# The mLSTM by chunks with a state, four GLA levels by blocks of 32 tokens, and another end of the program

## The chip, the core and the metric

The program runs on one core of a Trainium2 chip. The core has TensorE for matrix products (PE in the profile, PEld its weight loads), VectorE (DVE), ScalarE (ACT), GpSimd (POOL) and SyncE (SP), which issues most transfers. Each engine takes its own instructions in the order of the program, and the engines meet at semaphores. The metric is the device time of one launch in microseconds. Three runs of the kernel before gave 953.68, 954.08 and 954.04 us, median 954.04.

## What is computed

One decoder layer over 512 tokens of width 1024, all in float32: three token mixers side by side (mLSTM, GLA and gated DeltaNet, each with 4 heads of 128), merged by sigmoid gates, then a squared-ReLU MLP and a last RMSNorm. What the change touches, from the reference:

```python
def mlstm_chunk(carry, xs):                      # per head, chunk of tokens
    b = jnp.cumsum(lf, axis=-1)
    D = jnp.where(causal, b[..., :, None] - b[..., None, :] + li[..., None, :], -jnp.inf)
    inter = b + m[..., None]
    m_t = jnp.maximum(inter, jnp.max(D, axis=-1))
    P = jnp.exp(D - m_t[..., None]) * jnp.einsum('bhtk,bhsk->bhts', q, k)
    w_inter = jnp.exp(inter - m_t)
    num = jnp.einsum('bhts,bhsv->bhtv', P, v) + w_inter[..., None] * jnp.einsum('bhtk,bhkv->bhtv', q, C)
    den = jnp.sum(P, axis=-1) + w_inter * jnp.einsum('bhtk,bhk->bht', q, n)
    h = num / jnp.maximum(jnp.abs(den), jnp.exp(-m_t))[..., None]
    ...
    C = w_old[..., None, None] * C + jnp.einsum('bhsk,bhsv->bhkv', k * w_s[..., None], v)

def gla_chunk(S, xs):                            # a decay for each channel k
    b = jnp.cumsum(g, axis=2)
    diff = b[:, :, :, None, :] - b[:, :, None, :, :]
    decay = jnp.exp(jnp.where(causal[:, :, None], diff, -jnp.inf))
    A = jnp.einsum('bhtsk,bhsk->bhts', q[:, :, :, None, :] * decay, k)
    o = jnp.einsum('bhts,bhsv->bhtv', A, v) + jnp.einsum('bhtk,bhkv->bhtv', q * jnp.exp(b), S)

def rmsnorm(x, g):                               # the last one ends the program
    y = x32 * lax.rsqrt(jnp.mean(x32 * x32, axis=-1, keepdims=True) + EPS)
    return (y * g.astype(jnp.float32)).astype(x.dtype)
```

## The kernel before

Tokens stand on partitions or in columns in blocks of 128. Every large product (projections, gates, up and out projections, both MLP layers) is done as three matmuls of a high and a low float32r part, 128x128 weights by 512 columns; below they are called large matmuls. The small products of the mixers are plain float32, and each of their matmuls appears in the trace as two records; a transpose on TensorE (`tr`) appears as one.

The program is not written in the order in which it runs. `write_block` records operations in a graph, `Graph.schedule` places them by a planner with costs for each kind, and `emit` writes them out. The large matmuls come in the fixed order of `plan`. Everything else on TensorE is slipped between them, as what is called a visit here: a run of small float32 matmuls between two large ones. Small matmuls that wait for another engine are planned at least 1.5 us (`SLACK`) after their input. PSUM tiles of the small products come from a pool of 4 (`mps`). Since all operations are recorded by one helper, every row of the profile names the helper's line, and rows are told apart by tile names.

- mLSTM, `gen_mlstm(h)`: one causal product over all 512 tokens. For each block j of keys, `mqk` is one matmul of 512, 384, 256 or 128 columns (keys of block j by all later queries), `me` its weights exp(...) times the product. Then `mn` sums over the causal blocks: 1+2+3+4 = 10 matmuls of 129 columns (128 values and the normaliser).
- GLA, `gen_gla(h)`: inside a chunk of 128 the decay is split in seven levels, L = 64, 32, 16, 8, 4, 2, 1; each pairs the second half of a run of 2L tokens with its first half. `lw` holds the decayed keys, `lwq` the decayed queries, `ll` their product, which ends up in `lAT`. Levels 64, 32 and 16 are computed by runs (weights of 65, 33 or 17 columns). Levels 8, 4, 2 and 1 take, for each of 4 chunks, one matmul of 128 weight columns by 64 columns, and `copy_predicated` on VectorE picks what belongs to the level. The level of a head has its own PSUM tile.
- The gated DeltaNet, `gen_gdn`, goes chunk by chunk with a state already: `pks`, `pqs`, `pvn`, `pu`, `po`.
- The end, `mlp_last` and `finish(t)`: token blocks t = 0 to 3 get their last MLP product (`mop` for t = 2 and 3), are added to the residual in `x2`, squared with a sum on ScalarE (`fsq`), and scaled by y = 1/rms and the gain `gf`, and stored. The scaling of t = 0 to 2 is one VectorE instruction with both factors per half row (`x<-x,fy,gf`); for t = 3 the gain is multiplied ahead and y is applied on both engines.

Of the kernel before, what the change touches and what calls it, by code (L numbers as in the profile page):

```python
# [7 lines left out]
F32 = mybir.dt.float32  # L8
# [6 lines left out]
P = 128  # L15
D = 1024
S = 512
# [96 lines left out]
class Graph:  # L114
# [92 lines left out]
    def cost(self, eng, method, a, k, op):  # L207
# [10 lines left out]
        if eng == "tensor":  # L218
            if method == "transpose":
                return max(0.109, n / 1200), 0.2  # L220
            if a[1].t.dt == F32R:
                return max(0.112, n / 2400 + 0.0135), 0.2
            return 2 * max(a[1].shape[-1] / 1200, n / 1200, 0.012) + 0.007, 0.2
# [348 lines left out]
def write_block(nc, xT, w_cm, w_tm, w_sc, w_up, w_out, w_mi, w_mo, w_lr, prm, cst, g_fin, x_tm, out):  # L572
# [560 lines left out]
    def gen_mlstm(h):  # L1133
# [61 lines left out]
    hlT = []  # L1195
    cone = slot("cone")
# [8 lines left out]
    def gen_gla(h):  # L1205
        if h == 0:
# [3 lines left out]
            nc.gpsimd.memset(cone, 1.0)  # L1210
            nc.gpsimd.memset(h4(cone)[:, :, 0:1], 0.0)
# [33 lines left out]
        for li_, L in enumerate((64, 32, 16, 8, 4, 2, 1)):  # L1245
            nb = S // (2 * L)
            b3 = b.rearrange("p (n x) -> p n x", x=2 * L)
            w = nc.tile("w", [P, S], F32, f"lw{h}{L}")
            w3 = w.rearrange("p (n x) -> p n x", x=2 * L)
            k3 = lk[h].rearrange("p (n x) -> p n x", x=2 * L)  # L1250
            q3 = lq[h].rearrange("p (n x) -> p n x", x=2 * L)
            nc.vector.tensor_sub(w3[:, :, :L + 1], b3[:, :, L:L + 1].broadcast_to([P, nb, L + 1]), b3[:, :, :L + 1])
            if L > 1:
                nc.vector.tensor_sub(w3[:, :, L + 1:], b3[:, :, L + 1:], b3[:, :, L:L + 1].broadcast_to([P, nb, L - 1]))
            nc.scalar.activation(w, w, AF.Exp, scale=-1.0 / 16.0)
            q_ = q3[:, :, L:]
            if L > 1:
                wq = nc.tile("mq", [P, 256], F32, f"lwq{h}{L}").rearrange("p (n l) -> p n l", l=L)
                nc.vector.tensor_mul(wq, w3[:, :, L:], q_)
                q_ = wq  # L1260
            nc.vector.tensor_mul(w3[:, :, :L + 1], w3[:, :, :L + 1], k3[:, :, :L + 1])
            pl = mps(f"ll{h}{L}")
            p4 = pl[:, :256].rearrange("p (c n l) -> p c n l", c=4, l=L)
            nh = 64 // L
            if L >= 16:
                for c in range(4):
                    for i in range(nh):
                        o = c * P + i * 2 * L
                        mm(p4[i * 2 * L:i * 2 * L + L + 1, c, i], w[:, o:o + L + 1], q_[:, c * nh + i])
# [4 lines left out]
                for i in range(nh):  # L1274
                    r0 = i * 2 * L
                    nc.either.copy(A4[r0:r0 + L + 1, :, r0 + L:r0 + 2 * L], p4[r0:r0 + L + 1, :, i])
            else:
# [401 lines left out]
```

## Time and profile before

| | |
|---|---|
| median of 3 runs | 954.04 us |
| the profiled execution, its own time | 953.96 us |
| its span in the profile | 952.1 us |
| TensorE busy | 942.1 us, 99% |
| VectorE, ScalarE, GpSimd busy | 647.3, 458.5, 4.3 us |
| mean granted TensorE clock | 0.996 of full speed |
| last matmul starts | 942.9 us |

The chain that ended last, followed back from the last instruction, says which engine's work made the time. Along TensorE its pieces run from the start of one group to the start of the next, so that a piece's length by its count is the time that each record took of TensorE, while the durations of single matmuls overlap (a large matmul lasts 0.39 us and the next starts 0.23 us after it).

### The profile page before, as it was taken

How to read it: one execution, taken by the hardware profiler on the slowest of the kernel's cores; microseconds unless marked ns; L12 is line 12 of the kernel's file. 1: busy time of each engine (PE TensorE's matmuls, PEld its weight loads, DVE VectorE, ACT ScalarE, POOL GpSimd, SP SyncE). 2: the span in 40 equal slices, each digit the busy share in tenths (PEclk: the TensorE clock that was granted, in tenths of full speed). 3: DMA queues.
4: the chain of work that ended last, by engine and by line, in shares of the span. 5: the costliest groups of instructions: out<-in, count | busy, mean ns of one | idle time of the engine just before them, and what ended most of it. 6: DMA issues, size and time to landing. Idle time of an engine off the chain costs nothing.

```text
span 952.1 us, 12788 instructions
## 1 busy us (share of the span) xinstructions
PE 942.1 (99%) x4890; PEld 786.2 (83%) x4890; DVE 647.3 (68%) x1146; ACT 458.5 (48%) x877; POOL 4.3 (0%) x18
## 2 busy tenths in 40 slices
PE   9999999999999999999999999999999999999996
PEld 8888888888888888888888888888888888888885
DVE  6766766777725755877735754556778687876886
ACT  6545465543533664455333334455446446545533
POOL 0000000000000000000000000000000000000000
PEclk9999999999999999999999999999999999999998
DMA  9222524122411422222233223213241335424002
GB/s 347 107 90 102 164 89 133 56 78 89 119 67 45 178 89 89 89 67 67 90 111 111 89 94 105 89 45 115 87 149 60 122 111 177 134 88 133 1 1 89
DMA packets 37941, 96.74 MB, mean 102 GB/s; under 512 B 7884, under 2 KB 12108, under 8 KB 37880
## 3 DMA queue, kind: packets, MB, share of 16 engines
q1 hardware_dynamic: 37592, 95.62, 30.4%
q8 instruction: 38, 0.62, 0.3%
q10 hardware_dynamic: 288, 0.30, 0.1%
q14 instruction: 23, 0.19, 0.1%
HBM read 93.27 MB, written 2.65 MB: 101 GB/s over the span
## 4 chain that ended last, share of the span: by engine, by line
PE 99%; DVE 0%; DVEq 0%; issue 0%
PE mip L533 18%; PE pp L533 9%; PE upp L533 7%; PE P L533 6%; PE wop L533 5%; PE mop L533 3%; PE mvp L533 3%; PE lrp L533 2%; PE dzp L533 2%; PE lvp L533 2%; PE ll L533 2%; PE gt21p L533 1%; PE gt13p L533 1%; PE gt20p L533 1%; PE gt22p L533 1%; PE gt12p L533 1%
## 5 line engine op out<-in xcount | busy, mean ns | idle before, releaser
L533 DVE TENSOR_TENSOR em<-em 128x1024 f32<-128x1024 f32 x28 | 34.1, 1219 | 0.1
L533 ACT ACTIVATE A<-rl 128x256 f32<-128x256 f32 x64 | 23.7, 411 | 3.2 <-DVE aS4l L533 2.0
L533 DVE SCALAR_TENSOR_TENSOR sg<-sg,upp 128x512 f32<-128x512 f32 x24 | 16.5, 686 | 11.9 <-PE upp L533 11.7
L533 DVE TENSOR_TENSOR lw<-lbs 128x260 f32<-128x260 f32 (+12 forms) x52 | 20.9, 448 | 4.9 <-PE ll L533 4.9
L533 ACT ACTIVATE rl<-mip 128x512 f32<-128x512 f32 x32 | 18.9, 590 | 6.3 <-PE mip L533 6.3
L533 DVE TENSOR_TENSOR P<-P,pp 128x512 f32<-128x512 f32 x24 | 16.2, 686 | 7.6 <-PE pp L533 7.4
L533 ACT ACTIVATE lw<-lw 128x512 f32<-128x512 f32 x28 | 17.6, 630 | 7.9 <-DVE lw L533 7.3
L533 PEld LDWEIGHTS ll<-lwq,lw 128*17 128x17 f32 (+3 forms) x320 | 17.5, 131 | 3.8 <-ACT lAT L533 1.8
L533 PE MATMUL ll<-lwq,lw 128*17 128x16 f32 (+3 forms) x320 | 18.2, 214 | 0.0
L533 DVE SCALAR_TENSOR_TENSOR x<-pp,r2c,x 128x512 f32<-128x512 f32 x24 | 16.9, 745 | 0.0
L533 DVE TENSOR_TENSOR x2T<-xr,wop 128x512 f32<-128x512 f32 x8 | 5.5, 687 | 16.3 <-PE wop L533 16.3
L533 ACT ACT_TABLE_LOAD x10 | 12.8, 1283 | 1.3 <-PEq L1667 1.2
L533 DVE TENSOR_TENSOR lw<-lw,lks 128x260 f32<-128x260 f32 (+6 forms) x28 | 13.1, 497 | 0.0
L533 DVE SCALAR_TENSOR_TENSOR x<-pp,r2n,x 128x512 f32<-128x512 f32 x14 | 10.5, 748 | 3.1 <-PE pp L533 3.1
L533 ACT COPY lAT<-ll 17x64 f32<-17x64 f32 (+3 forms) x32 | 7.1, 231 | 10.8 <-PE ll L533 10.4
L533 ACT ACTIVATE yh<-sg 128x512 fp32r<-128x512 f32 x8 | 5.0, 632 | 13.5 <-DVE sg L533 13.5
L533 DVE TENSOR_TENSOR me<-me,mqk 128x512 f32<-128x512 f32 (+3 forms) x16 | 7.7, 484 | 5.4 <-PE mqk L533 4.9
L533 ACT ACTIVATE fsq<-x 128x512 f32<-128x512 f32 (+1 forms) x9 | 5.3, 585 | 12.5 <-DVE x L533 12.5
L533 PEld LDWEIGHTS mn<-mv,me 128*128 128x128 f32 x80 | 10.0, 191 | 1.1 <-DVE smo L533 0.2
L533 DVE TENSOR_TENSOR sg<-sg,sg 128x512 f32<-128x512 f32 x16 | 10.8, 690 | 0.1
L533 PE MATMUL mqk<-mqs,mks 128*128 128x512 f32 (+3 forms) x32 | 10.7, 432 | 0.0
L533 ACT ACTIVATE cvs<-cv 128x512 f32<-128x512 f32 x12 | 7.5, 629 | 6.1 <-DVE cv L533 6.0
(1849 smaller groups left out, 3276.1 us busy)
## 6 DMA issues: line engine op xcount, KB each, us to landing
em<-in_w_mo_dram SPq DMA_DIRECT2D x28, 512.0 KB, 3.3
xk<-in_xT_dram SPq DMA_DIRECT2D x8, 256.0 KB, 5.3
em<-in_x_tm_dram SPq DMA_DIRECT2D x4, 512.0 KB, 8.4
em<-scr_rows SPq DMA_DIRECT2D x16, 128.0 KB, 5.0
xr<-in_xT_dram SPq DMA_DIRECT2D x8, 256.0 KB, 4.0
out_dram<-x SPq DMA_DIRECT2D x7, 256.0 KB, 2.4
nm<-scr_rows SPq DMA_DIRECT2D x4, 256.0 KB, 4.6
mo00r<-in_w_tm_dram SPq DMA_DIRECT2D x1, 512.0 KB
```

Of the source, the lines that this page charges most:

```text
L533: getattr(getattr(nc, eng), method)(*[f(x) for x in a], **{n: f(x) for n, x in k.items()})
```

## The change

1. `gen_mlstm` keeps the causal product inside each chunk of 128 and carries a state `C` from chunk to chunk. Per head: a transpose of three chunks of the keys (`mkt`), scaled on VectorE into `kt`; four `mqk` of 128 columns into one PSUM tile; three `mu` = keys by values of 129 columns; `C` built from `mu` by one copy and two VectorE instructions; the queries scaled by exp in `qe`; and 4 + 3 = 7 `mn` instead of 10. Small scalars of the state go through `x` (`mx`). The rows of exp and of the masks are as long as before for the blocks that remain.
2. `gen_gla` goes through the levels in the groups (64), (32, 16), (8, 4), (2, 1); the levels of a group share a PSUM tile. Levels 8 to 1 are 16 matmuls of 32 weight columns by 16 columns instead of 4 of 128 by 64: each reaches its own 32 partitions of the result. What they don't write is read by `copy_predicated`, so that ScalarE copies zeros into the PSUM tile first (512 columns, two per head). `nc.after` lets a group's products begin when the keys of its last level are there.
3. The end: t = 0 and 1 get the gain on GpSimd and y on ScalarE (`nc.scalar.mul`) instead of both on VectorE; a square root on a single column (`root`) ahead brings the table load forward.
4. The planner's cost of a small matmul of at most 16 columns by at most 33 weight columns is 0.033 us. The planner's order of all engines changes with this.

```diff
+            if n <= 16 and a[1].shape[-1] <= 33:
+                return 0.033, 0.2
...
-        pt = []
-        for j in range(4):
-            e = nc.tile("w", [P, S], F32, f"me{h}{j}")
-            bias = a_c[:, h, j:j + 1]
-            nc.scalar.activation(e[:, blk(j)], md[:, blk(j)], AF.Exp, bias=bias)
-            if j < 3:
-                nc.scalar.activation(e[:, (j + 1) * P:], nm[:, (j + 1) * P:], AF.Exp, bias=bias)
-            pq = mps(f"mqk{h}{j}")
-            mm(pq[:, j * P:], mk[h][:, blk(j)], mq[h][:, j * P:])
-            nc.vector.tensor_mul(e[:, j * P:], e[:, j * P:], pq[:, j * P:])
-            pt.append(e)
+
+        end = h4(nm)[:, :, P - 1]
+        x = small("mx", 16)
+        nc.vector.tensor_add(x[:, 0:3], a_c[:, h, 0:3], end[:, 0:3])
+        nc.vector.tensor_sub(x[:, 3:5], end[:, 1:3], end[:, 0:2])
+        nc.vector.tensor_scalar_mul(x[:, 8:11], end[:, 0:3], -1.0)
+        nc.scalar.activation(x[:, 0:5], x[:, 0:5], AF.Exp)
+        kt, e, qe, C = (nc.tile("w", [P, S], F32, f"m{n}{h}") for n in ("kt", "e", "qe", "C"))
+
+        pk = mps(f"mkt{h}")
+        for c in range(3):
+            tr(pk[:, blk(c)], mk[h][:, blk(c)])
+        nc.vector.tensor_mul(h4(kt)[:, :3], h4(pk)[:, :3], bc(x[:, 0:3]))
+        for c in range(4):
+            nc.scalar.activation(e[:, blk(c)], md[:, blk(c)], AF.Exp, bias=a_c[:, h, c:c + 1])
+        pq = mps(f"mqk{h}")
+        for c in range(4):
+            mm(pq[:, blk(c)], mk[h][:, blk(c)], mq[h][:, blk(c)])
+        nc.vector.tensor_mul(e, e, pq)
+        for c in range(1, 4):
+            nc.scalar.activation(qe[:, blk(c)], nm[:, blk(c)], AF.Exp, bias=x[:, 7 + c:8 + c])
+        nc.vector.tensor_mul(qe[:, P:], qe[:, P:], mq[h][:, P:])
+        pu = mps(f"mu{h}")
+        for c in range(3):
+            mm(pu[:, blk(c, P + 1)], kt[:, blk(c)], mv[c][:, h, :])
+        nc.either.copy(C[:, :P + 1], pu[:, :P + 1])
+        for c in (1, 2):
+            nc.vector.scalar_tensor_tensor(C[:, blk(c, P + 1)], C[:, blk(c - 1, P + 1)], x[:, 2 + c:3 + c], pu[:, blk(c, P + 1)], op0=ALU.mult, op1=ALU.add)
...
-                for j in range(t + 1):
-                    mm(n2[:, tt], pt[j][:, blk(t)], mv[j][:, h, :], start=(j == 0), stop=(j == t))
+                mm(n2[:, tt], e[:, blk(t)], mv[t][:, h, :], start=True, stop=(t == 0))
+                if t:
+                    mm(n2[:, tt], qe[:, blk(t)], C[:, blk(t - 1, P + 1)], start=False, stop=True)
...
+    zero = slot("zero", n=512)
...
+            nc.gpsimd.memset(zero, 0.0)
...
-        for li_, L in enumerate((64, 32, 16, 8, 4, 2, 1)):
+        for levels in ((64,), (32, 16), (8, 4), (2, 1)):
...
+            pl = mps(f"ll{h}{levels[0]}")
+            if levels[0] < 16:
+
+                nc.scalar.copy(pl[:, :256 * len(levels)], zero[:, :256 * len(levels)])
+
+            def prod(o, a, q_):
+
+                nc.after(lw[levels[-1]])
+                mm(o, a, q_)
...
+                    else:
+                        for i in range(4):
+                            n0 = c * nh + i * m
+                            prod(p4[blk(i, 32), c, i * m:(i + 1) * m], w[:, blk(4 * c + i, 32)], q_[:, n0:n0 + m])
...
-                for c in range(4):
-                    mm(p4[:, c], w[:, blk(c)], q_[:, c * nh:(c + 1) * nh])
-                nc.vector.copy_predicated(At.rearrange("p (c n x) -> p c n x", c=4, x=2 * L)[:, :, :, L:], lmask(li_ - 3), p4)
...
+                    nc.vector.copy_predicated(At.rearrange("p (c n x) -> p c n x", c=4, x=2 * L)[:, :, :, L:], lmask((8, 4, 2, 1).index(L)), p4)
...
+            if t < 2:
+                nc.gpsimd.tensor_mul(o, o, gf[hf])
...
-                nc.vector.scalar_tensor_tensor(x2[t][hf], x2[t][hf], y, gf[hf], op0=ALU.mult, op1=ALU.mult)
+                if t < 2:
+                    nc.scalar.mul(x2[t][hf], x2[t][hf], y)
+                else:
+                    nc.vector.scalar_tensor_tensor(x2[t][hf], x2[t][hf], y, gf[hf], op0=ALU.mult, op1=ALU.mult)
...
+    root = small("root", 1)
+    nc.follow(prev[1][1])
+    nc.scalar.activation(root, r2c[:, 0:1], AF.Sqrt)
```

How the built programs stand, without times. In both, 3705 large matmuls follow in the same order of stages. Before there are 104 visits of small matmuls among them, after 111.

**TensorE, one visit with small GLA levels of heads 0, 1 and 2, before.** `ll` is the PSUM tile, `lw` the weights, `lwq` or `lqs` the queries; 128x64 is the shape of the result; the large matmuls around it are of the gate projection.

```order
L533 MATMUL ll_4203<-lqs_2293,lw_3828 128x64
L533 MATMUL ll_4205<-lwq_4145,lw_4124 128x64 x4
L533 MATMUL ll_4203<-lqs_2293,lw_3828 128x64 x2
L533 MATMUL ll_4218<-lwq_4165,lw_4130 128x64 x4
L533 MATMUL ll_4227<-lqs_2335,lw_4021 128x64
L533 MATMUL ll_4203<-lqs_2293,lw_3828 128x64
L533 MATMUL ll_4227<-lqs_2335,lw_4021 128x64 x3
```

The same engine after, at level 8 and level 4 of head 0: one group of 16 between large matmuls, and the next split by level 64 of head 1.

```order
L535 MATMUL gt13p_3864<-xh,gt130h 128x512
L535 MATMUL ll_3849<-lwq_3412,lw_3358 32x16 x16
L535 MATMUL gt13p_3864<-xh,gt130l 128x512
...
L535 MATMUL ll_3849<-lwq_3836,lw_3365 32x16 x11
L535 MATMUL ll_3957<-lwq_3917,lw_3861 65x64 x4
L535 MATMUL ll_3957<-lqs_2364,lks_2945 1x1 x4
L535 MATMUL ll_3849<-lwq_3836,lw_3365 32x16 x5
```

There are 16 such groups of 16 in the program, in 16 visits, four of which hold other small matmuls too; the 64 matmuls of 128x64 are gone.

**TensorE, the first head's mLSTM, before:** products of all later queries, then (30 rows on) the sums over blocks.

```order
L533 MATMUL mqk_1442<-mqs_1319,mks_861 128x512
L533 MATMUL mqk_1450<-mqs_1319,mks_861 128x384
L533 MATMUL mqk_1455<-mqs_1319,mks_861 128x256
...
L533 MATMUL mn_1539<-mv_111,me_1420 128x129
L533 MATMUL mn_1539<-mv_113,me_1428 128x129
L533 MATMUL mn_1539<-mv_115,me_1433 128x129
```

The same engine after:

```order
L535 MATMUL mkt_1353<-cs,mks_861 128x128 x3
L535 MATMUL mkt_1358<-cs,mks_904 128x128 x3
L535 MATMUL mq0p_1317<-xh,mq01l 128x512
...
L535 MATMUL mqk_1378<-mqs_1325,mks_861 128x128 x4
...
L535 MATMUL mu_1401<-mv_111,mkt_1366 128x129
L535 MATMUL mu_1401<-mv_113,mkt_1366 128x129
L535 MATMUL mu_1401<-mv_115,mkt_1366 128x129
```

Six large matmuls stand between `mkt` and `mqk`, three between `mqk` and `mu`, some nine more until the first `mn`.

**ScalarE, the end of the program, before.** x_5438, x_5614, x_5426 and x_5602 are the halves of t = 0 and 1; x_5433 and x_5609 of t = 2, x_5455 and x_5631 of t = 3.

```order
L533 ACTIVATE fsq,fss<-x_5602 128x512
L533 ACTIVATE fsq,fss<-x_5433 128x512
L533 ACT_TABLE_LOAD
L533 ACTIVATE fs<-fss,fe 128x1 x2
L533 ACTIVATE fsq,fss<-x_5609 128x512
L533 ACTIVATE fs<-fss,fe 128x1
L533 ACTIVATE fsq,fss<-x_5455 128x512
```

The same engine after; x_5664, x_5840, x_5652 and x_5828 are now the halves of t = 0 and 1, x_5659 and x_5835 of t = 2, x_5681 of t = 3:

```order
L535 ACTIVATE fs<-fss,fe 128x1 x2
L535 ACTIVATE fsq,fss<-x_5659 128x512
L535 ACTIVATE x_5664<-x_5664,fy 128x512
L535 ACTIVATE x_5840<-x_5840,fy 128x512
L535 ACTIVATE x_5652<-x_5652,fy 128x512
L535 ACTIVATE fsq,fss<-x_5835 128x512
L535 ACTIVATE x_5828<-x_5828,fy 128x512
```

Four multiplications by y stand on ScalarE among the squares, and four fewer on VectorE; the table load moved ahead of the first square. On GpSimd, the four multiplications by the gain follow an ISA instruction (a reload of its library) that the program before does not have. ScalarE also has 14 table loads instead of 10, the four new ones in the softplus of the GLA: two beside the `lvp` and two beside the `dzp` projection.

## Rows read from the trace of the kernel before

**Rows 1.** The page: busy us, share of span, instructions; shares of the chain.

```profile
PE 942.1 (99%) x4890; PEld 786.2 (83%) x4890; DVE 647.3 (68%) x1146; ACT 458.5 (48%) x877; POOL 4.3 (0%) x18
...
PE 99%; DVE 0%; DVEq 0%; issue 0%
```

**Rows 2.** TensorE's waits: who waited for whom, us, times, longest.

```profile
PE mvp L533 <- DVE onem L533: 1.1, 1, 1.1
```

**Rows 3.** Chain, MLP: start us, us until the next piece, what, records.

```profile
646.57 5.44 PE mip L533 x24
```

**Rows 4.** Chain, mLSTM, 154 to 191 us: single products, one head's sums.

```profile
154.80 0.86 PE mqk L533 x2
...
171.84 0.65 PE mqk L533 x2
...
175.66 0.43 PE mqk L533 x2
...
176.78 0.22 PE mqk L533 x2
...
188.65 2.23 PE mn L533 x20
```

**Rows 5.** Chain: four transposes; two steps of the DeltaNet's state.

```profile
157.05 0.44 PE pk L533 x4
...
287.78 0.89 PE pvn L533 x8
288.67 1.38 PE upp L533 x6
```

**Rows 6.** Chain, GLA levels and the large matmuls behind them.

```profile
394.88 0.32 PE ll L533 x32
395.19 1.59 PE gt22p L533 x6
...
412.25 0.74 PE ll L533 x16
...
440.50 3.52 PE ll L533 x32
444.02 6.90 PE gt21p L533 x30
```

**Rows 7.** Chain, 32x32 matmuls of the DeltaNet's solve.

```profile
260.16 1.13 PE pY L533 x64
261.29 3.62 PE gt20p L533 x15
264.91 1.03 PE pT L533 x29
```

**Rows 8.** Stretch of the GLA levels, 385 to 475 us: length, busy of each engine.

```profile
385.00:475.00 90.00, 90.00 (x689) 74.90 (x688) 71.79 (x146) 42.07 (x86) 2.04 (x4) 1.00 0.24 77
```

**Rows 9.** Timeline of the end: start us, us, engine, operation, count, idle time before.

```profile
924.87 0.64 ACT L533 ACTIVATE fsq<-x 128x512 f32<-128x512 f32 x1 [1.33 <-DVE x L533]
...
933.00 0.63 ACT L533 ACTIVATE fsq<-x 128x512 f32<-128x512 f32 x1 [1.94 <-DVE x L533]
...
939.60 0.73 DVE L533 SCALAR_TENSOR_TENSOR x<-x,fy,gf 128x512 f32<-128x512 f32 x1
...
943.24 0.48 DVE L533 SCALAR_TENSOR_TENSOR x<-mop,r2c,x 128x256 f32<-128x256 f32 x1 [0.23 <-PE mop L533]
...
946.40 1.79 DVE L533 SCALAR_TENSOR_TENSOR x<-x,fy,gf 128x512 f32<-128x512 f32 x3
...
946.52 0.72 ACT L533 ACTIVATE x<-x,fy 128x512 f32<-128x512 f32 x1 [1.93 <-DVE fy L533]
...
948.11 0.35 DVE L533 TENSOR_SCALAR x<-x,fy 128x256 f32<-128x256 f32 x1
```

**Rows 10.** Chain, two of the small steps of y at the end.

```profile
944.36 0.15 DVE fv L533
...
945.57 0.18 DVE fs L533
```

More of the change, by code (lines that the diff above doesn't have):

```diff
@@ L1244, in gen_gla @@
         nc.either.copy(lkt[h][:, :3 * P], pk[:, :3 * P])
-        for li_, L in enumerate((64, 32, 16, 8, 4, 2, 1)):
[L1246 to L1265, printed above, removed]
-                for c in range(4):
-                    for i in range(nh):
-                        o = c * P + i * 2 * L
-                        mm(p4[i * 2 * L:i * 2 * L + L + 1, c, i], w[:, o:o + L + 1], q_[:, c * nh + i])
@@ new lines, in gen_gla @@
+        for levels in ((64,), (32, 16), (8, 4), (2, 1)):
+            lw, lq_ = {}, {}
+            for L in levels:
+                nb = S // (2 * L)
+                b3 = b.rearrange("p (n x) -> p n x", x=2 * L)
+                w = nc.tile("w", [P, S], F32, f"lw{h}{L}")
+                w3 = w.rearrange("p (n x) -> p n x", x=2 * L)
+                k3 = lk[h].rearrange("p (n x) -> p n x", x=2 * L)
+                q3 = lq[h].rearrange("p (n x) -> p n x", x=2 * L)
+                nc.vector.tensor_sub(w3[:, :, :L + 1], b3[:, :, L:L + 1].broadcast_to([P, nb, L + 1]), b3[:, :, :L + 1])
+                if L > 1:
+                    nc.vector.tensor_sub(w3[:, :, L + 1:], b3[:, :, L + 1:], b3[:, :, L:L + 1].broadcast_to([P, nb, L - 1]))
+                nc.scalar.activation(w, w, AF.Exp, scale=-1.0 / 16.0)
+                q_ = q3[:, :, L:]
+                if L > 1:
+                    wq = nc.tile("mq", [P, 256], F32, f"lwq{h}{L}").rearrange("p (n l) -> p n l", l=L)
+                    nc.vector.tensor_mul(wq, w3[:, :, L:], q_)
+                    q_ = wq
+                nc.vector.tensor_mul(w3[:, :, :L + 1], w3[:, :, :L + 1], k3[:, :, :L + 1])
+                lw[L], lq_[L] = w, q_
+            pl = mps(f"ll{h}{levels[0]}")
[4 more added lines that the diff above has]
+                mm(o, a, q_)
+            for n, L in enumerate(levels):
+                w, q_ = lw[L], lq_[L]
+                p4 = pl[:, blk(n, 256)].rearrange("p (c n l) -> p c n l", c=4, l=L)
+                nh, m = 64 // L, 16 // L
+                for c in range(4):
+                    if L >= 16:
+                        for i in range(nh):
+                            o = c * P + i * 2 * L
+                            prod(p4[i * 2 * L:i * 2 * L + L + 1, c, i], w[:, o:o + L + 1], q_[:, c * nh + i])
+                    else:
+                        for i in range(4):
+                            n0 = c * nh + i * m
+                            prod(p4[blk(i, 32), c, i * m:(i + 1) * m], w[:, blk(4 * c + i, 32)], q_[:, n0:n0 + m])
@@ L1273, in gen_gla @@
                     nc.either.copy(A4[0:1, :, 0:1], pl[0:1, 256:260].unsqueeze(2))
[L1274 to L1277, printed above, removed]
-                for c in range(4):
-                    mm(p4[:, c], w[:, blk(c)], q_[:, c * nh:(c + 1) * nh])
-                nc.vector.copy_predicated(At.rearrange("p (c n x) -> p c n x", c=4, x=2 * L)[:, :, :, L:], lmask(li_ - 3), p4)
+                if L >= 16:
+                    for i in range(nh):
+                        r0 = i * 2 * L
+                        nc.either.copy(A4[r0:r0 + L + 1, :, r0 + L:r0 + 2 * L], p4[r0:r0 + L + 1, :, i])
+                else:
+                    nc.vector.copy_predicated(At.rearrange("p (c n x) -> p c n x", c=4, x=2 * L)[:, :, :, L:], lmask((8, 4, 2, 1).index(L)), p4)
     lss = one("lss", [P, 16])
@@ L1579, in finish @@
             for hf in range(2):
-                nc.vector.scalar_tensor_tensor(x2[t][hf], x2[t][hf], y, gf[hf], op0=ALU.mult, op1=ALU.mult)
+                if t < 2:
+                    nc.scalar.mul(x2[t][hf], x2[t][hf], y)
+                else:
+                    nc.vector.scalar_tensor_tensor(x2[t][hf], x2[t][hf], y, gf[hf], op0=ALU.mult, op1=ALU.mult)
                 nc.sync.dma_start(out[blk(t), blk(hf, 512)], x2[t][hf])
```

## The prediction

> **What bounds the kernel now.** I read the chain of work that ended last first. TensorE holds 99% of it, and TensorE is busy for 942.1 of the 952.1 us of the span [rows 1]. Busy can hide waits behind long matmuls, so the list of TensorE's waits comes second: it has one entry, 1.1 us at the start [rows 2]. Third come the chain's pieces in the MLP: 24 large matmuls take 5.44 us, 0.2267 us each, without a break [rows 3]. So TensorE is never late for anything, and the time is what TensorE's instructions cost, one after the other, plus what follows the last matmul. A change of TensorE's own work is paid one to one; work on other engines counts only where it makes TensorE wait, or behind the last matmul.
>
> That last stretch is 943.2 to 952.1 us. VectorE works there without a pause on leftovers: from 943.24 until 948.11 + 0.35 = 948.46 us it has the last addition, two multiplications by the gain, four scalings of half rows of t = 1 and 2, and t = 3's own [rows 9]. The last store is issued behind it; the other 3.6 us of the span are that store and the end of the program.
>
> I make the sum against the profiled execution's own 953.96 us; the median of the runs is 954.04, so the two are one number here.
>
> **The mLSTM.** A piece of the chain with its count gives TensorE's price of a record. Before, per head: the four products cost 0.86, 0.65, 0.43 and 0.22 us, together 2.16, and the ten sums 2.23 us for 20 records, 0.1115 each [rows 4]. After, per head: four products of 128x128 are 8 records. Such a record costs 0.89 / 8 = 0.111 us in the DeltaNet's state [rows 5], so 0.89 us. Three transposes cost 3 x 0.11 = 0.33 us [rows 5]. Three `mu` of 129 columns are 6 records, 0.67 us, and seven `mn` are 14 records, 1.56 us, both at the 0.1115 of [rows 4]. That is 3.45 us instead of 4.39, **0.94 us less a head, 3.8 us in all**. The bounds are narrow, 3.5 to 4.0, since every shape stands in the trace.
>
> Around it, VectorE and ScalarE lose some long instructions and gain about as many short ones; neither bounds anything. What it could cost is a wait: keys transposed, scaled, multiplied, `C` built, and only then the sums, four steps over three engines where two stood before. The trace has the same kind of chain in the DeltaNet: there the large matmuls right behind a visit cost 1.38 us for six, 0.23 each, so no wait follows [rows 5], and the list of waits has none there [rows 2]. Six, three and about nine large matmuls lie between a step and the next for the first head; at 0.2267 us that is 1.4, 0.7 and 2 us of cover. I take nothing for it in the sum and keep it as a rival.
>
> **The GLA's four small levels.** Before, the 128 records of 128 weight columns by 64 cost 3.52 us for 32, plus an edge: the thirty large matmuls behind them take 6.90 us instead of 30 x 0.2267 = 6.80. So 3.6 us for a head's 32, 14.4 us in all [rows 6]. After, 512 records of 32 weight columns by 16, in 16 visits of 32. The trace has not this shape, but level 16 comes near: 32 records with 17 weight columns by 16 columns, in the same order over the four groups of 32 partitions. They cost 0.32 us (the piece at 394.88), and the six large matmuls behind them 1.59 instead of 1.36: 0.55 us with the edges [rows 6]. 16 x 0.55 = 8.8 us. Four of the visits share their edges with others, which I leave as an allowance for 32 instead of 17 weight columns. **5.6 us less.** The lower bound of the cost is 0.52 a visit (edges shared), 6.1 us less. The upper one is the row where only two tiles alternate: `pY`, 32x32, costs 1.13 + (3.62 - 3.40) = 1.35 us for 64 records [rows 7], of which the 0.22 is edge, so 0.79 for 32, 12.6 in all: 1.8 us less. I take level 16's price, since its tiles, rows and moving columns are the same and only the weight columns differ.
>
> The Trainium skill has a rule that speaks against this step ("TensorEngine Tiling (Array Packing)", Performance Considerations, Instruction Overhead): a matmul has some 60 cycles of overhead, so that one column lasts as long as sixty, and a dimension that is already small should give no tiling factor. By it 512 short records would each cost an estimated 25 ns and the step would bring next to nothing; level 16's 0.32 us for 32 records is 10 ns each and speaks against the rule here.
>
> Hidden beside TensorE: eight copies of zeros into PSUM on ScalarE, about 0.6 us each by its other instructions of 512 columns [rows 9], 4.7 us more in a stretch where ScalarE is busy for 42.07 of 90 us. VectorE has 71.79 us there and keeps its work [rows 8]; with 5.6 us less of TensorE the stretch is 84.4 us long and VectorE 85% busy. That still covers it; the margin is what the waiting rival eats. The four table loads that ScalarE gains lie beside the `lvp` and `dzp` projections, where hardly a visit stands on TensorE and the wait list is empty [rows 2].
>
> **The end.** Behind the last matmul VectorE keeps the last addition (0.48), one gain multiplication of 256 columns (about the 0.35 of the row of 256), one scaling of 512 (0.73), t = 3's small steps (0.15 and 0.18 in [rows 10], with two reciprocals and a sum that are no longer, some 0.5), and the last half row (0.4 and 0.35): 2.8 us from 943.24, so 946.05 instead of 948.46 [rows 9]. That is 2.4 us. ScalarE's own scaling of t = 3 starts with the same y and ends near 946.2, and two stores of 256 KB then start at once instead of half a microsecond apart, so I take **2.1 us less**, with bounds 0 and 2.4. It rests on t = 0 and 1 being out of the way: GpSimd's multiplications can start with the first square at 924.87 and the last of the four at 933.63 [rows 9], 18 and 10 us ahead of the last matmul's end; the trace has no arithmetic on GpSimd, so I bound it from below by VectorE's 0.73 us for a scaling of as many elements [rows 9], and take twice that. The four scalings on ScalarE, 0.72 us each, fit between its squares, where it idles 1.9 us at a time [rows 9].
>
> **Sum.** 3.8 + 5.6 + 2.1 = 11.5 us; 953.96 - 11.5 = **942.5 us**. With all bounds at their good ends, 4.0 + 6.1 + 2.4, it is 941.5, with the levels' cost at its upper bound 946.3, and with the end's gain gone as well 948.4.
>
> **Rivals.** *TensorE comes to wait.* The mLSTM has 12 new hand-overs and the levels 8 with ScalarE's zeros. If half of them wait for one VectorE instruction of about 0.45 us, 4.5 us come back: 947.0. Against it: today's list of waits is empty with a chain of the same kind in it; for it: the cover of three large matmuls is only 0.7 us.
>
> *The short matmuls don't overlap as level 16's.* Single-column matmuls on one tile show what a short record costs alone: in the 0.74 us of 16 records [rows 6] eight have 64 columns and eight have one; at half of `mqk`'s 0.111 for the former, 0.04 us is left for each of the latter with the edges, 0.025 to 0.035. At 0.03 us, 512 records cost 15.4 us and 16 edges 0.23 each 3.7: 4.7 us more than before in place of 5.6 less, in all 952.8. That would be within 0.2% of before or just faster; the row `pT`, all on one tile, has the same 0.035 us a record [rows 7]. Against it: level 16 has four tiles in turn and 0.010.
>
> *GpSimd is late (slower than before).* ScalarE takes its instructions in order, and the scalings of t = 0 and 1 stand ahead of the squares of t = 2 and 3. If GpSimd's first product comes late, all that ends the program comes late with it. Cover: t = 0 is scaled from 939.60 now, behind the table load that moves ahead, so from some 3 us earlier then; from the first square's end, 925.5, to 936.5, less GpSimd's own 1.4, leaves some 9 us [rows 9]. Each further microsecond is paid in full, and with the 11.5 us won elsewhere the kernel is slower than before from 20 us on; 25 us late gives 958.5. For it: the program now reloads GpSimd's library, which the trace does not price. Against it: the reload stands in GpSimd's queue behind work of the GLA, some 500 us earlier, and may run there. The Trainium skill ("GPSIMD Engine Reference", Instruction dispatch) gives about 6 us for the first call of a freshly loaded kernel; no run here shows it, and it would be covered.
>
> **How the numbers follow.** The forecast, 941.0 to 944.5, has 0.67; waiting, around 947, 0.15; levels between level 16's price and the bound of `pY`, up to 948.4, 0.08; no overlap, about 952.8, 0.04; GpSimd late, 958, 0.04; anything else 0.02. The range is 941.0 to 947.5. A measurement of this kernel tells about 0.2%, 1.9 us, from no change. Faster by more than that: 0.67 + 0.15 + 0.08 + a share of the rest = 0.92; the same 0.04; slower 0.04.
>
> **What would show it.** In the trace after: TensorE's list of waits still almost empty; the visits of 32 `ll` records 0.32 us long as level 16's; eight `mqk` records 0.89 us; the last matmul near 933.8 us; VectorE's last instruction 2.8 us behind it. Wrong it would be if TensorE waits anywhere for more than a microsecond, if an `ll` record costs over 0.02 us, or if ScalarE stands before a scaling of t = 0 or 1 near the end.

## The result, and the profile after

The changed kernel takes 943.31 us (median of four runs, 943.29 to 943.96); the kernel before, beside it, 953.92 us. The ratio is 0.9891, with an interval of 0.9873 to 0.9908: faster, by 10.6 us or 1.1%. The prediction was 942.5 us, range 941.0 to 947.5.

The page after, with the lines that answer to [rows 1]: busy time, share and instructions of each engine, and the shares of the chain that ended last.

```profile
span 941.5 us, 13618 instructions
...
PE 932.8 (99%) x5286; PEld 775.3 (82%) x5286; DVE 651.4 (69%) x1157; ACT 469.6 (50%) x903; POOL 10.7 (1%) x23
...
PE 97%; DVE 2%; ACT 0%; DMA 0%; issue 0%; SPq 0%; DVEq 0%
```

TensorE's waits after, the answer to [rows 2] (who waited for whom, us, times, longest):

```profile
PE mvp L535 <- DVE onem L535: 1.1, 1, 1.1
```

TensorE is busy 9.3 us less, 932.8 for 942.1, although it has 396 records more. Its list of waits still holds the one entry at the start, so none of the new hand-overs is waited for. VectorE's share of the chain went from 0% to 2%: the chain leaves TensorE earlier than it did, at the program's end, which is shown below.

The chain in the mLSTM after (start us, us until the next piece, what, records), the answer to [rows 4]:

```profile
140.01 0.89 PE mqk L535 x8
...
142.26 2.08 PE dk1p L535 x9
144.34 0.45 PE mn L535 x4
...
146.37 0.22 PE mn L535 x2
...
147.30 0.67 PE mu L535 x6
...
148.66 0.33 PE mkt L535 x3
...
151.06 0.89 PE mn L535 x8
```

These are the prediction's prices to the hundredth: four products 0.89, three transposes 0.33, three `mu` 0.67, and 14 records of `mn` 0.45 + 0.22 + 0.89 = 1.56. The sum of a head is 3.45 us, where it was 4.39.

The chain in the GLA after, the answer to [rows 6]:

```profile
418.37 0.32 PE ll L535 x32
...
421.65 0.38 PE ll L535 x32
422.03 1.59 PE gt12p L535 x6
...
435.32 0.92 PE ll L535 x48
...
449.09 1.01 PE ll L535 x45
```

The piece of 0.32 is a level 16, as before. The next one is a level 8 to 1 in its new form: 0.38 us for 32 records, and the six large matmuls behind it cost 1.59 instead of 1.36, so 0.61 with the edge where the prediction took 0.55. The pieces of 48 and 45 records are two of the four visits in which such a level stands with another and pays no edge of its own. 16 x 0.61 less four edges of 0.23 is 8.8 us, the predicted sum: what a visit costs more is what the shared edges give back. The allowance for this was not worked out, so that the two come out equal is luck.

The end, three engines' timelines of the changed kernel (start us, us, engine, operation, count, idle time before and what ended it). First GpSimd and ScalarE:

```profile
916.43 1.55 POOL L535 TENSOR_TENSOR x<-x,gf 128x512 f32<-128x512 f32 x1 [531.47 <-ACT fsq L535]
920.03 1.52 POOL L535 TENSOR_TENSOR x<-x,gf 128x512 f32<-128x512 f32 x1 [2.05 <-ACT fsq L535]
```

```profile
928.17 0.63 ACT L535 ACTIVATE fsq<-x 128x512 f32<-128x512 f32 x1 [0.18 <-DVE x L535]
928.71 0.19 ACT L535 ACTIVATION_READ_ACCUMULATOR fsq<-x 128x1 f32 x1
928.93 1.95 ACT L535 ACTIVATE x<-x,fy 128x512 f32<-128x512 f32 x3
930.79 0.61 ACT L535 ACTIVATE fsq<-x 128x512 f32<-128x512 f32 x1
```

And VectorE, which answers to [rows 9, 10]:

```profile
916.75 1.78 DVE L535 TENSOR_TENSOR z01l<-A,z01h 128x512 fp32r<-128x512 f32 x1
...
919.71 0.68 DVE L535 TENSOR_TENSOR z11l<-A,z11h 128x512 fp32r<-128x512 f32 x1
920.32 1.78 DVE L535 SCALAR_TENSOR_TENSOR x<-u,r2c,x 128x512 f32<-128x512 f32 x1
...
923.88 3.48 DVE L535 SCALAR_TENSOR_TENSOR x<-P,r2c,x 128x512 f32<-128x512 f32 x3
927.28 0.20 DVE L535 TENSOR_SCALAR fe<-fss 128x1 f32<-128x1 f32 x2
927.40 0.73 DVE L535 SCALAR_TENSOR_TENSOR x<-mop,r2c,x 128x512 f32<-128x512 f32 x1
...
929.07 0.73 DVE L535 SCALAR_TENSOR_TENSOR x<-mop,r2c,x 128x512 f32<-128x512 f32 x1
931.53 0.16 DVE L535 TENSOR_TENSOR fv<-fss,fe 128x1 f32<-128x1 f32 x1 [1.73 <-ACT fsq L535]
931.61 0.74 DVE L535 SCALAR_TENSOR_TENSOR x<-mop,r2c,x 128x512 f32<-128x512 f32 x1
...
934.70 0.48 DVE L535 SCALAR_TENSOR_TENSOR x<-mop,r2c,x 128x256 f32<-128x256 f32 x1
...
936.21 0.15 DVE L535 TENSOR_TENSOR fv<-fss,fe 128x1 f32<-128x1 f32 x1
...
936.98 0.48 DVE L535 SCALAR_TENSOR_TENSOR x<-x,fy,gf 128x256 f32<-128x256 f32 x1
937.38 0.35 DVE L535 TENSOR_SCALAR x<-x,fy 128x256 f32<-128x256 f32 x1
```

The last matmul starts at 933.70 and ends at 933.98, where before it ended at 943.20: 9.2 us earlier. From there to the span's end are 7.5 us, where there were 8.95: 1.45 us less, together the span's 10.7. VectorE's last addition starts 0.73 us behind the last matmul (before 0.04), and two things stand ahead of it. At 916.75 and 920.32, while GpSimd multiplies, instructions of VectorE take 1.78 us that took 0.68 and 0.74 before. At 928.93 ScalarE has three scalings of t = 0 and 1 ahead of the second square of t = 2, whose input was there at 929.8. VectorE waits 1.73 us for that square, and the addition for t = 3 stands behind the wait.

Both lie on the chain that ended last. Before, it stays on TensorE until the last matmul; after, it leaves TensorE at 914.80 and goes on over VectorE's stretched instruction ("issue" is time in which the engine waits for nothing that the profile shows), ScalarE's scalings and the square:

```profile
932.17 11.04 PE mop L533 x60
943.22 0.02 issue
```

```profile
911.84 2.96 PE P L535 x13
...
916.84 0.06 DVE z01l L535
916.89 1.56 issue
...
929.57 1.32 ACT x L535 x2
930.89 0.62 ACT fsq L535 x2
```

### The profile page after: what moved, and what is told of

Its sections match the earlier page's. It is cut to its first block, busy times and chain, and to the rows that moved or that the text cites. A ratio compares the mean times of both kernels' runs of the same rounds, so it can differ in the third digit from the quotient of the medians.

```text
span 941.5 us, 13618 instructions
## 1 busy us (share of the span) xinstructions
PE 932.8 (99%) x5286; PEld 775.3 (82%) x5286; DVE 651.4 (69%) x1157; ACT 469.6 (50%) x903; POOL 10.7 (1%) x23
## 4 chain that ended last, share of the span: by engine, by line
PE 97%; DVE 2%; ACT 0%; DMA 0%; issue 0%; SPq 0%; DVEq 0%
PE mip L535 19%; PE pp L535 10%; PE upp L535 7%; PE P L535 5%; PE wop L535 5%; PE lrp L535 3%; PE mvp L535 2%; PE lvp L535 2%; PE dzp L535 2%; PE mop L535 2%; PE ll L535 1%; DVE x L535 1%; PE gt12p L535 1%; PE gt21p L535 1%; PE gt22p L535 1%; PE gt13p L535 1%
## 5 line engine op out<-in xcount | busy, mean ns | idle before, releaser
L535 PEld LDWEIGHTS ll<-lwq,lw 128*32 128x32 f32 (+3 forms) x608 | 9.4, 109 | 6.9 <-issue 5.3
L535 DVE COPY_PREDICATED lAT<-cs,ll 128x256 f32<-128x256 uint8 x16 | 9.3, 583 | 5.3 <-PE ll L535 5.3
L535 ACT COPY lAT<-ll 17x64 f32<-17x64 f32 (+3 forms) x32 | 7.0, 231 | 10.6 <-PE ll L535 10.3
L535 POOL TENSOR_TENSOR x<-x,gf 128x512 f32<-128x512 f32 x4 | 5.9, 1484 | 535.9 <-ACT fsq L535 535.9
L535 PE MATMUL ll<-lwq,lw 128*32 128x16 f32 (+3 forms) x608 | 11.5, 187 | 0.0
L535 DVE TENSOR_TENSOR sg<-sg,sg 128x512 f32<-128x512 f32 x16 | 10.7, 686 | 0.1
L535 DVE TENSOR_TENSOR lwq<-lw,lqs 128x256 f32<-128x256 f32 x24 | 9.8, 423 | 0.3
L535 DVE TENSOR_TENSOR Z<-Z,tmU 64x30 f32<-64x30 f32 (+14 forms) x30 | 9.5, 318 | 0.2
```

The costliest lines, as they stand in the source:

```text
L535: getattr(getattr(nc, eng), method)(*[f(x) for x in a], **{n: f(x) for n, x in k.items()})
```

## The experiments

Theory: three parts, each paid one to one (the first two by TensorE's visits, the third by the distance from the last matmul to the end), and small records cheap because records on different quarters of the array overlap. Rivals: the gain comes from another order of the planner; from the grouping of the levels; the price of a record is its issue or its columns; and for the end, GpSimd's stretch or ScalarE's queue as what kept it short.

The kernels, with the median, the ratio to the kernel before and its interval, and the time from the last matmul's end to the span's end:

| kernel | us | ratio (interval) | behind the last matmul |
|---|---|---|---|
| changed | 943.31 | 0.9891 (0.9873 to 0.9908) | 7.50 |
| old mLSTM | 946.79 | 0.9925 (0.991 to 0.994) | 7.50 |
| old GLA levels | 948.67 | 0.9946 (0.9931 to 0.996) | 7.50 |
| old end | 944.74 | 0.9906 (0.989 to 0.9923) | 8.93 |
| same quarter in a row | 950.59 | 0.9965 (0.9952 to 0.9978) | 7.52 |
| groups, old shapes | 949.02 | 0.9949 (0.9933 to 0.9966) | 7.46 |
| blocks of 64 | 946.75 | 0.9925 (0.9913 to 0.9937) | 7.52 |
| early root alone | 944.45 | 0.9901 (0.9887 to 0.9916) | 8.32 |
| scalings moved | 943.17 | 0.9888 (0.9874 to 0.9901) | 6.99 |
| no product on GpSimd (t = 0 and 1 miss the gain) | 942.71 | 0.9885 (0.9871 to 0.9898) | 6.99 |
| gain on VectorE | 943.33 | 0.9891 (0.9875 to 0.9906) | 7.18 |
| three edits of the end | 942.75 | 0.9885 (0.987 to 0.99) | 6.87 |

Kernels that differ in the end alone end their last matmul between 933.93 and 934.23 us with the same plan for TensorE, so that 0.3 us between two times says nothing of an edit; the last column is steadier.

### One part undone at a time

The mLSTM, as it was:

```diff
-        pu = mps(f"mu{h}")
-        for c in range(3):
-            mm(pu[:, blk(c, P + 1)], kt[:, blk(c)], mv[c][:, h, :])
...
+                for j in range(t + 1):
+                    mm(n2[:, tt], pt[j][:, blk(t)], mv[j][:, h, :], start=(j == 0), stop=(j == t))
```

> The changed kernel with the mLSTM of before (one causal product over all 512 tokens); the GLA's blocks and the new end stay. If the three parts of the change are paid one to one and add up, the time is that of the changed kernel, 943.3 us, plus the 3.8 us of TensorE's visits (bounds 3.5 to 4.0): 947.1 us, and the distance from the last matmul to the end stays 7.5 us. Rival: the chunked mLSTM's gain on TensorE was given back or came from the new order of the large matmuls; then the time stays within 0.7 us of 943.3.

946.79 us, 3.5 more. The distance at the end is unchanged. Its chain has the old prices back, a product of 512 columns and one of 384 among them:

```profile
150.18 0.86 PE mqk L535 x2
...
154.46 0.65 PE mqk L535 x2
```

The rival is out. Of the 3.8 by the prices some 0.3 are missing; the last matmul's end varies by as much between kernels of one plan, and no run says where they went.

The GLA's levels, as they were:

```diff
-        for levels in ((64,), (32, 16), (8, 4), (2, 1)):
+        for li_, L in enumerate((64, 32, 16, 8, 4, 2, 1)):
...
-                            prod(p4[blk(i, 32), c, i * m:(i + 1) * m], w[:, blk(4 * c + i, 32)], q_[:, n0:n0 + m])
+                    mm(p4[:, c], w[:, blk(c)], q_[:, c * nh:(c + 1) * nh])
```

> The changed kernel with the GLA's levels of before (seven levels each with its own PSUM tile, levels 8 to 1 by 128 weight columns and 64 columns, no zeros); mLSTM and end stay as changed. The trace of the changed kernel has 17.8 us for all visits of the levels, that of before 23.3: expected 943.3 + 5.5 = 948.8 us. If the prediction's lower price of a level were the right one it would be 949.4, by its upper one 945.1. Rival: the shorter matmuls brought nothing that the trace's piece lengths can be trusted for; then 943.3.

948.67 us: 5.4 more, between the two bounds and by the level 16's price.

The end, as it was:

```diff
-            if t < 2:
-                nc.gpsimd.tensor_mul(o, o, gf[hf])
...
-                if t < 2:
-                    nc.scalar.mul(x2[t][hf], x2[t][hf], y)
-                else:
-                    nc.vector.scalar_tensor_tensor(x2[t][hf], x2[t][hf], y, gf[hf], op0=ALU.mult, op1=ALU.mult)
+                nc.vector.scalar_tensor_tensor(x2[t][hf], x2[t][hf], y, gf[hf], op0=ALU.mult, op1=ALU.mult)
...
-    nc.scalar.activation(root, r2c[:, 0:1], AF.Sqrt)
```

> The changed kernel with the end of before: VectorE scales t = 0 and 1 with both factors, no product on GpSimd, no scaling of them on ScalarE, no early square root. Last matmul to the end of the span was 8.95 us before and 7.5 us after, so 943.3 + 1.45 = 944.8 us; the prediction's term would give 945.4. Rival: the new end gained nothing of its own (the shorter distance came from the planner's other order): 943.3.

944.74 us, 1.4 more, and the distance is back at 8.93. So the end's part is worth 1.4 us. The three parts undone come to 3.5 + 5.4 + 1.4 = 10.3 of the 10.6: they add up.

### What makes a small record cheap

The same 512 records, the quarter in the outer loop:

```diff
-                for c in range(4):
...
-                        for i in range(4):
+                    for i in range(4):
+                        for c in range(4):
                             n0 = c * nh + i * m
```

> The changed kernel with the same 512 records of levels 8 to 1, but in another order: all four chunks of one group of 32 partitions first, then the next group, so that eight records in a row use the same quarter of the array. If a record is cheap because records on different quarters overlap, it now costs what pT's on one tile cost, 0.035 us: 32 x 0.035 + 0.23 = 1.35 us a visit instead of 0.585, 16 visits 12 us more, about 955.5 us. If a record costs only what its issue costs (7 ns by the changed kernel's trace), the order changes nothing: 943.3. If only the two records of one matmul must follow each other and neighbours overlap anyway, something near the latter.

950.59 us, 7.3 more with not an instruction added. In its chain, the same visits:

```profile
400.62 0.81 PE ll L535 x32
...
420.14 0.32 PE ll L535 x32
...
423.42 0.82 PE ll L535 x32
```

Level 16, in its old order, still costs 0.32; a level of the new form went from 0.38 to 0.81 or 0.82, and 16 x 0.44 = 7.0 us is the loss. A record costs 0.025 us on the average of the piece, with quarters in turn 0.012.

The starts of the single records, which the rows above merge, show why (the visit at 421.58 in the changed kernel's trace, the one at 423.35 in this run's). In both, two records on the same quarter start 0.032 us apart (the first two 0.053). In the changed kernel four quarters run side by side, 0.007 us behind one another, so that four records start every 0.032 us. Here the next quarter's first record starts 0.153 us behind this one's first, when three of its eight are still to start. So the overlap is what pays, and the expectation's mechanism is right. Its price for one quarter was nearly right too: `pT`'s records start 0.032 us apart as well, and its 0.035 is the same with the ends of the piece. What it left out is that quarters still overlap where they change.

The Trainium skill's 60 cycles of overhead for a matmul ("TensorEngine Tiling (Array Packing)", Performance Considerations, Instruction Overhead), an estimated 25 ns, come near this run's average for a record (half of a matmul of the program). But neither pace in the two traces is 25 ns: it is 32 ns on one quarter and 7 ns between quarters in turn. So the rule does not hold here for tiles in turn, and for one tile its figure is low.

The new groups of levels with the old shapes:

```diff
-                        for i in range(4):
-                            n0 = c * nh + i * m
-                            prod(p4[blk(i, 32), c, i * m:(i + 1) * m], w[:, blk(4 * c + i, 32)], q_[:, n0:n0 + m])
+                        prod(p4[:, c], w[:, blk(c)], q_[:, c * nh:(c + 1) * nh])
```

> The changed kernel with the levels in their new groups (shared PSUM tiles, zeros, the wait for the last keys of a group), but levels 8 to 1 by the matmuls of before, 128 weight columns by 64 columns. If the GLA's gain is the price of the short matmuls, it all goes: 16 visits of 0.90 us instead of 0.585 are 5 us more, 948.4 us, as with the whole old GLA. If part of it came from the grouping (fewer visits, fewer edges), the time lies below that; if all of it, 943.3.

949.02 us, 5.7 more: as slow as the whole old GLA. The same visit in its chain:

```profile
425.89 0.84 PE ll L535 x8
```

Grouping, zeros and the wait for the last keys bring nothing by themselves; the short matmuls bring all.

Blocks of 64 tokens:

```diff
-                        for i in range(4):
-                            n0 = c * nh + i * m
-                            prod(p4[blk(i, 32), c, i * m:(i + 1) * m], w[:, blk(4 * c + i, 32)], q_[:, n0:n0 + m])
+                        for i in range(2):
+                            n0 = c * nh + i * 2 * m
+                            prod(p4[blk(i, 64), c, i * 2 * m:(i + 1) * 2 * m], w[:, blk(2 * c + i, 64)], q_[:, n0:n0 + 2 * m])
```

> The changed kernel with levels 8 to 1 by blocks of 64 tokens: 8 matmuls of 64 weight columns by 32 columns for a level, 16 records a visit, two halves of the array in turn, instead of 32 records of 32 by 16 on four quarters. If a record's price is its issue and the pair of halves overlap as pY's two tiles, 16 x 0.0177 + 0.22 = 0.50 us a visit instead of 0.585: 1.3 us less, 942.0 us. If the price follows the columns that the array works on (0.11 us for a record of 128 by 64, so 0.055 for 32 columns and half of that with two in turn), 16 x 0.0275 + 0.2 = 0.64 us: 0.9 us more, 944.2. If two halves in turn do not overlap, 16 x 0.055 + 0.2 = 1.08 us a visit: 8 us more, 951.

946.75 us, 3.4 more, and none of the three times came. A visit's piece in its chain, and the six large matmuls behind it:

```profile
427.85 0.59 PE ll L535 x16
428.44 1.59 PE gt12p L535 x6
```

The price in the second case was right all the same. In the trace two records on one half start 0.058 us apart and the other half's run beside them, 0.029 us a record: a full overlap of the two halves. What the expectation left out is the start and the end of the piece: it set 16 x 0.0275 + 0.2 = 0.64 against 0.585, where the whole visit costs 0.59 and 0.23 of edge, 0.82, against 0.61 in the changed kernel. 16 x 0.21 is 3.4 us.

For a level the piece is 0.84 us with 128 by 64 (as in the run with the old shapes), 0.59 with 64 by 32 and 0.38 with 32 by 16. On one tile the records start 0.112, 0.058 and 0.032 us apart, and one, two or four tiles run side by side. That pace goes with the weight columns: `pT`, with 32 weight columns by 32, has the 0.032 of 32 by 16, and `mqk`, with 128 by 128, the 0.111 of 128 by 64. The old matmuls of a level paid for 128 weight columns, of which each column of queries needed few.

### What kept the end short

Three of ScalarE's scalings behind the square of t = 2's second half row:

```diff
             square_of(t, o)
+            if (t, hf) == (2, 1):
+                for s in scal[1:]:
+                    s.soft = [nc.ops[-1]]
```

> The changed kernel with one edit of the order: on ScalarE three of the four scalings of t = 0 and 1 are placed behind the square of the second half row of t = 2 (in the changed kernel three stand ahead of it, and VectorE waits 1.73 us for that square with the addition for t = 3 behind the wait). If ScalarE's queue is what kept the end's gain 0.65 us below the predicted 2.1 us, VectorE's wait goes, the scaling of t = 2 moves up, and the last addition starts at the last matmul's end again: 0.5 to 0.7 us less, 942.7 us, with 6.9 us from the last matmul to the end of the span. Rival: VectorE, stretched by GpSimd's products, is late anyway: within 0.2 us of 943.3.

VectorE's wait fell from 1.73 to 0.79 us, and the last addition moved from 0.73 to 0.2 us behind the last matmul. In its timeline:

```profile
930.73 0.16 DVE L535 TENSOR_TENSOR fv<-fss,fe 128x1 f32<-128x1 f32 x1 [0.79 <-ACT fsq L535]
931.27 0.75 DVE L535 SCALAR_TENSOR_TENSOR x<-mop,r2c,x 128x512 f32<-128x512 f32 x1 [0.39 <-PE mop L535]
...
934.30 0.48 DVE L535 SCALAR_TENSOR_TENSOR x<-mop,r2c,x 128x256 f32<-128x256 f32 x1
```

The distance is 6.99 us, half a microsecond less, as expected. The median, 943.17, is only 0.14 below, since the last matmul ended 0.13 later and the rest is within what the runs vary by. So the queue is shown by the trace, not by the time.

Without GpSimd's products:

```diff
-            if t < 2:
-                nc.gpsimd.tensor_mul(o, o, gf[hf])
```

> The changed kernel without GpSimd's four products of t = 0 and 1 by the gain (this part of the result is left out: those two token blocks miss the gain). If GpSimd's products stretch VectorE's instructions that have two inputs in SBUF, the VectorE instructions of 916 to 927 us that took 1.78 us take 0.75 or less, the first addition of t = 2 starts 8.2 us ahead of the last matmul's end instead of 6.6, and the time is 0.5 to 1 us less: 942.3 to 942.8. Rival: that stretch is VectorE's own and stays, or it is hidden: 943.3, first addition 6.6 us ahead.

VectorE's timeline, the same three groups of instructions as above:

```profile
916.10 0.68 DVE L535 TENSOR_TENSOR z01l<-A,z01h 128x512 fp32r<-128x512 f32 x1
...
920.88 0.74 DVE L535 SCALAR_TENSOR_TENSOR x<-u,r2c,x 128x512 f32<-128x512 f32 x1
...
922.94 2.07 DVE L535 SCALAR_TENSOR_TENSOR x<-P,r2c,x 128x512 f32<-128x512 f32 x3
```

0.68, 0.74 and 2.07 us instead of 1.78, 1.78 and 3.48: GpSimd's products cost VectorE 3.55 us, and the first addition of t = 2 is 8.27 us ahead of the last matmul's end instead of 6.57. The time, 942.71 us, lies in the expected range too. But the planner's order changed with it and has both squares of t = 2 ahead of all scalings, and the distance is 6.99 us, the same as with the products and ScalarE mended. So the stretch is real, and where ScalarE is not in the way it is hidden: in both these runs the chain stays on TensorE, until 931.25 with the products and 931.07 without, and taking the stretch off brings nothing further. What the stretch alone costs with ScalarE's order of the changed kernel, where it lies on the chain, is not shown: no run has that order without the products.

The gain on VectorE, early, and t = 2 scaled between the additions:

```diff
-                nc.gpsimd.tensor_mul(o, o, gf[hf])
+                nc.vector.tensor_mul(o, o, gf[hf])
+                gain.append(nc.ops[-1])
...
+            if (t, hf) == (3, 0):
+                nc.soft = gain[2:]
+            if (t, hf) == (3, 1):
+                nc.soft = y2[c0 // 256:c0 // 256 + 1]
```

> The changed kernel with another end: VectorE itself multiplies t = 0 and 1 by the gain, early, between the last additions (0.6 us each where GpSimd's product took 1.5 and stretched VectorE by 1.0), ScalarE squares t = 2 ahead of all four scalings by y, and VectorE scales t = 2 between the last three additions. Nothing is left out. If both findings at the end hold, VectorE's last instruction ends some 2.6 us behind the last matmul instead of 3.75: 1.0 to 1.2 us less, 942.2 us. Rival: VectorE has no room for 2.4 us more work before the last matmul ends, additions come late, and the time is that of the changed kernel or up to 1 us more.

943.33 us, the rival's outcome by the time. VectorE has no room: its last addition starts 0.66 us behind the last matmul again, now behind a gain of t = 3 and a scaling of t = 2. Its last instruction ends 3.49 us behind the last matmul where 2.6 was expected, so that by the distance, 7.18, 0.3 of the 1.0 to 1.2 us came.

Only the early square root, with the old end:

```diff
-                if t < 2:
-                    nc.scalar.mul(x2[t][hf], x2[t][hf], y)
...
     nc.scalar.activation(root, r2c[:, 0:1], AF.Sqrt)
```

> The changed kernel with the end of before except for the early square root that brings ScalarE's table load forward: VectorE scales t = 0 and 1 with both factors, nothing on GpSimd. In the run with the whole old end the table load stood from 927.2 to 928.5 us, VectorE's chain for t = 0 and 1 waited for it, and its first scaling began at 930.35. If the load is what makes VectorE's leftovers late, most of the end's 1.45 us come back: 943.5 us. If the leftovers are too much work for VectorE whatever the load does, the root brings 0 to 0.5 us: 944.2 to 944.7.

944.45 us, the second alternative by the time: 0.3 us less than with the whole old end. By the distance, 8.32 instead of 8.93, the early table load is worth 0.6 us of the end's 1.43, a little more than that alternative allowed, and the work taken off VectorE the other 0.8.

Three edits together:

```diff
+                half[0].soft = [add_]
...
-            if t < 2:
+            if t < 2 or (t, hf) == (2, 1):
                 nc.gpsimd.tensor_mul(o, o, gf[hf])
...
-                if t < 2:
+                if t < 2 or hf:
                     nc.scalar.mul(x2[t][hf], x2[t][hf], y)
```

> The changed kernel with three edits of the end, nothing left out: ScalarE's scalings of t = 0 and 1 behind the square of t = 2's second half row, as in the run that moved them (distance from the last matmul to the end of the span 6.99 us instead of 7.5); t = 2's second half row takes the gain on GpSimd and y on ScalarE, so that VectorE has one scaling less behind the last matmul; and VectorE does the gain of t = 3's first half row behind the last addition instead of ahead of it. In the run with the moved scalings the last addition began 0.2 us late and VectorE's normalisation waited 0.48 us behind that scaling of t = 2. If these are what is left, the distance falls by another 0.3 to 0.6 us to about 6.5, and the time is 942.4 to 942.7 us. Rival: a fifth product on GpSimd stretches VectorE where it is late, or ScalarE is now the late one: 943.2 or more.

942.75 us, the lowest of the kernels that compute everything, 0.56 below the changed kernel; the intervals of the two overlap, so it is not shown to be faster. The last addition starts 0.04 us behind the last matmul, and yet the distance is 6.87 and not 6.5: the gain that was put behind the addition now stands ahead of the small sum `fe`, for which ScalarE's root waits.

```profile
934.24 0.49 DVE L535 SCALAR_TENSOR_TENSOR x<-mop,r2c,x 128x256 f32<-128x256 f32 x1 [0.36 <-PE mop L535]
934.64 0.68 DVE L535 TENSOR_TENSOR x<-x,gf 128x512 f32<-128x512 f32 x1
935.24 0.21 DVE L535 TENSOR_SCALAR fe<-fss 128x1 f32<-128x1 f32 x1
```

## Why the prediction was right, step by step

- **The bound.** TensorE is never late, so its own work is paid one to one: right. The last matmul was forecast near 933.8 us and ended at 933.98; the list of waits is unchanged.
- **The mLSTM**, 3.8 us: the prices of all four kinds of pieces came out as read, and undoing the part costs 3.5 us, the lower bound.
- **The GLA's levels**, 5.6 us: 5.4 when undone. Level 16 was the right row. A visit cost 0.06 us more than taken, and the four shared edges, left as an allowance for just that, covered it.
- **The end**, 2.1 us: 1.45 by the trace, 1.4 when undone. This term was mis-sized, by 0.65 us; VectorE's last instruction, forecast to end 2.8 us behind the last matmul, ended 3.75 behind it. The prediction let VectorE's last addition start with the last matmul's end, as before, and had ScalarE's four scalings "fit between its squares". They did not: its squares of t = 2 came late (the first at 928.17, in the run without GpSimd's products at 926.44), three scalings went ahead of one of them, and the last addition started 0.73 us late. That VectorE stands while GpSimd multiplies was not in the sum at all. Moving the scalings gave 0.5 us back. Another 0.27 is in the small steps of y, from the first at 936.21 to the last half row at 936.98: 0.77 us where 0.5 was taken. The 0.3 us by which the term was held below VectorE's own 2.4 covered part of the two.
- **Rivals.** TensorE waiting: no new wait. No overlap of the short matmuls: the run with the same quarter in a row comes nearest to it. The pace on one quarter, 0.032 us, lies in the rival's 0.025 to 0.035; the average is 0.025 since quarters overlap where they change, so that the time is 950.6 and not 952.8. A record at 25 ns, which by the prediction would bring next to nothing, loses: this run takes 1.9 us more than the one with the old levels, for the edges come on top. GpSimd late: its first product starts at 916.43, 0.08 us behind the end of the first square's sum, and takes 1.55 us, where twice 0.73 was taken; no late first call stands there. The reload's two instructions stand in the trace at 384.9, where the prediction placed them; what may have followed them had 531 us to end. But the mechanism of this rival, ScalarE in order with the scalings ahead of the squares, is the one whose mending gave the half microsecond back, without GpSimd being late.

## What to carry to other kernels

When TensorE bounds a kernel and never waits, price a change of its small matmuls by whole pieces of the chain with the same shape and the same order of tiles, and add one edge for each visit; that was good to a few tenths of a microsecond here, while the price of a record without the ends of its piece missed by 2.5 us (blocks of 64). Small matmuls pay when neighbours lie on different parts of the array: the order of two loops was worth 7 us. Where work is moved from a late engine to one that works in order, list what will stand behind it there, at the time at which it will really run, and what the engine that was to be relieved does meanwhile.

## What the runs showed of the hardware

- 32 records of 32 weight columns by 16 columns cost 0.38 us with four quarters in turn, and 0.81 with eight records in a row on each quarter. With halves in turn, 16 records of 64 by 32 cost 0.59. On one tile records start 0.032, 0.058 and 0.112 us apart with 32, 64 and 128 weight columns (with 64 and 128 moving columns alike at 128), and tiles in turn run side by side.
- While GpSimd multiplies two tiles of 512 columns in SBUF (1.35 to 1.55 us), an instruction of VectorE with both inputs in SBUF doesn't slow down, it stands: the two at 916.75 and 920.32 end at 918.53 and 922.10, each 0.55 us behind the end of GpSimd's product (917.98 and 921.55), which is somewhat less than the 0.68 and 0.74 that they take without. The single instructions of the group at 923.88 say the same: its last two, with both inputs in SBUF, take 1.12 and 1.77 us and end 0.55 us behind the third and the fourth product, while its first, which reads a product of TensorE's from PSUM, runs beside the third and takes 0.74. The Trainium skill says so ("SBUF — State Buffer", SBUF: two separate sides): the two engines share a pair of ports that one holds for a whole instruction while the other is blocked. The trace agrees, with 1.0 to 1.1 us for each of the two at 916.75 and 920.32; the prediction had not priced it, and four products cost VectorE 3.55 us, more than the four multiplications would have cost VectorE itself at 0.6 each.
